# Twelve of x's sixteen row blocks turned by VectorE in 32x32 blocks, features of x and rows of w_in in another order, weights split two row blocks at a time

## The chip, the cores and the metric

The kernel runs on one core of a Trainium2 chip. A core has five engines, each with its own queue of instructions that it takes in order: TensorE (PE, matmul), VectorE (DVE), ScalarE (ACT), GpSimd (POOL) and SyncE (SP), and 16 DMA engines that carry what SP, ACT and POOL issue. The metric is the time of one execution on the device in microseconds (us). Smaller is better.

## The reference

One layer of a bidirectional encoder trunk on x of 512 tokens by 2048 features, all in float32:

```python
h = rms_norm(x, norm_w)                       # x * rsqrt(mean(x*x) + 1e-6) * norm_w
proj = jnp.einsum('bsd,de->bse', h, w_in)     # 2048 -> 4608 columns
q, k, v, g_attn, xr, g_lru = jnp.split(proj, SPLITS, axis=-1)
attn_out = attention_group(q, k, v, q_norm_w, k_norm_w)
lru_out = lru_group(xr, conv_w, conv_b, lru_wa, lru_ba, lru_wx, lru_bx, lru_lambda)
mixed = jnp.concatenate([rms_norm(attn_out, attn_norm_w) * jax.nn.silu(g_attn),
                         rms_norm(lru_out, lru_norm_w) * jax.nn.silu(g_lru)], axis=-1)
return x + jnp.einsum('bse,ed->bsd', mixed, w_out)
```

What matters here is the start: every column of `proj` is a sum over all 2048 features, so PE needs x with features on the 128 partitions (turned), and w_in with the same features on the same partitions. The order of the features is free as long as both have the same one. The factor `rsqrt(mean)` belongs to a token and is multiplied in after the matmul.

## The kernel before

**Numbers in two halves.** A float32 operand is split into a high half (rounded to the fast float32 form of PE) and a low half (the rest). A product takes three matmuls: high by high, high by low, low by high (`mm3`, lines 151 to 154: L152, L153, L154 in the profile). The high half of the weights is written by ACT (`wsplit`, L224), the low half by DVE as a subtraction (L226), each for one row block of 128 features and 512 columns, into four buffers `wh` and four `wl`.

**Chunks.** w_in is loaded in chunks of two row blocks (256 features) by 512 columns, 512 KB each (`wraw`, L203, on SP's queue), into three buffers `wr`. A projection of 512 columns goes over 8 chunks and accumulates in four PSUM banks `pj`; a chunk is 24 matmuls of 512 columns. A bank is free again when its content has been multiplied by `rbc` and stored in SBUF (`evac_bc`, L427), or scaled by `rstd` (L552).

**x.** During the first projection (columns of xr, `C_XR`) x itself is loaded and turned, chunk by chunk: `xload` (L245) brings 512 tokens by 256 features, four blocks of 128 tokens on the partitions. `xturn` lets PE turn each row block with four transpositions of 128x128 (L256) into one PSUM bank, from which ACT writes the high half, scaled by norm_w (L258), and DVE the low half (L259). `xsquare` lets DVE square the chunk and add up per token (L269). The turned halves `xh` and `xl` stay in SBUF for all later projections.

**Statistics.** When all chunks are in, `xstats` adds the sums (L306), POOL takes mean and power -0.5 (L286, L287) for `rstd`, four values per partition. In `rows` PE turns them into a row (L298), DVE copies it (L299), and POOL's queue stores it to DRAM (L301) and loads it back to all partitions as `rbc` (L302).

**What sets the order.** PE's order is that of the program text (a manual schedule for the whole kernel), as are SP's order during the first projection, POOL's up to the query projections, and ACT's and DVE's up to chunk 2. Beyond, a scheduler orders ACT and DVE by priority and its own estimate of times. In the loop of the first projection (the code is at the end of the listing) the generators `loads` and `turns` set where the loads and the turning of the later chunks are issued between PE's steps.

**Later stages.** After the first projection come a second one of xr beside the first half of the recurrence, keys and values, queries (with further buffers in a pool `wx`), then the gates beside the attention. The gate stage goes over a plan of units: `gl_units` (gate of the recurrence, in the seven products of a Strassen-like scheme, with 12 matmuls of 512 columns per chunk, some weights being sums that were put in DRAM by `two_gl` and accumulating DMAs on POOL's queue) and `ga_units` (gate of the attention, half as many columns, one of the four buffers `wh` for two row blocks). The last stage is the output projection with w_out, which has its own operands.

## Time and profile before

| | |
|---|---|
| Median of 3 runs | 642.55 us (642.46 to 642.91) |
| Span of the profiled execution | 640.7 us |
| What lies around the span, against the median | 1.85 us |
| Busy in the span: PE, DVE, ACT, POOL | 636.0, 509.9, 382.2, 131.7 us |
| First matmul of the second projection | 56.7 us after the span's start |

The profiled execution's own time is given as its span, from the first instruction to the end of the last one. Times of the timeline count from the span's start. In a row of the timeline the first number is the start and the second the length; in a row of a group stand the count, the busy time and the mean length of one in ns. A row of the stretches has, after the stretch's length, the busy time of PE, PE's weight loads, DVE, ACT and POOL, then TensorE's granted clock, the share of the DMA engines and GB/s.

### The profile page before, as it was taken

Reading aid. Unit: us, or ns where it says so; the run is one execution under the profiler, and the core shown is the slowest. Engines: PE = TensorE matmul, PEld = TensorE weight load, DVE = VectorE, ACT = ScalarE, POOL = GpSimd, SP = SyncE. Lnnn points to the kernel's source line nnn. Section 1 sums busy time; section 2 is a strip of 40 time slices with the busy share of each in tenths; the row PEclk is TensorE's granted clock in tenths of the full one; section 3 lists DMA queues with packets and bytes.
Section 4 is the critical chain, followed back from the end, with each engine's and each line's share of the span. In section 5 each row is a group of like instructions: output and inputs, shape, how many; then the busy total and the mean of one; then the engine's idle time right before and its main releaser. Section 6 shows DMA issues by size and latency. Waiting matters only on the chain.

```text
span 640.7 us, 8950 instructions
## 1 busy us (share of the span) xinstructions
PE 636.0 (99%) x2962; PEld 528.3 (82%) x2962; DVE 509.9 (80%) x886; ACT 382.2 (60%) x725; POOL 131.7 (21%) x173
## 2 busy tenths in 40 slices
PE   9999999999999999999999999999999999999997
PEld 7888888888888888888888888888888888888886
DVE  5777679996698994977678877559938988698994
ACT  3543799489954624877666775946444754344441
POOL 0013403222150501412444353322000000110000
PEclk9999999999999999999999999999999999999999
DMA  8847976897757646445989997875565857585322
GB/s 295 293 140 202 242 203 154 247 252 182 186 158 196 203 135 196 137 141 162 239 241 280 252 253 225 196 209 149 131 196 204 295 175 248 185 281 208 122 93 99
DMA packets 68782, 128.19 MB, mean 200 GB/s; under 512 B 5504, under 2 KB 24320, under 8 KB 68480
## 3 DMA queue, kind: packets, MB, share of 16 engines
q1 hardware_dynamic: 55856, 90.25, 43.2%
q0 software_dynamic: 12704, 37.23, 25.3%
q8 instruction: 23, 0.38, 0.2%
q14 instruction: 23, 0.19, 0.1%
q10 hardware_dynamic: 176, 0.14, 0.1%
HBM read 119.21 MB, written 41.95 MB: 252 GB/s over the span
## 4 chain that ended last, share of the span: by engine, by line
PE 99%; DVE 0%; issue 0%
PE pj L152 19%; PE pj L153 19%; PE pj L154 19%; PE mm L1008 13%; PE pj L1008 11%; PE mm L152 3%; PE mm L154 3%; PE mm L153 3%; PE mm L655 2%; PE mm L256 1%; PE pj L332 1%; PE pj L349 1%; PE mm L591 1%; PE mm L1253 1%; PE mm L1047 0%; PE mm L741 0%
## 5 line engine op out<-in xcount | busy, mean ns | idle before, releaser
L224 ACT CAST wh<-wr 128x512 fp32r<-128x512 f32 x151 | 90.1, 618 | 70.6 <-PE pj L154 25.4
L226 DVE TENSOR_TENSOR wl<-wr,wh 128x512 fp32r<-128x512 f32 (+1 forms) x153 | 105.6, 713 | 30.9 <-ACT wh L224 29.6
L152 PE MATMUL pj<-x,wh 128*128 128x512 f32 x240 | 95.1, 396 | 0.0
L152 PE MATMUL pj<-wh,x 128*128 128x512 f32 x240 | 93.9, 391 | 0.0
L154 PE MATMUL pj<-x,wl 128*128 128x512 f32 x240 | 93.5, 390 | 0.0
L153 PE MATMUL pj<-x,wh 128*128 128x512 f32 x240 | 93.5, 390 | 0.0
L154 PE MATMUL pj<-wh,x 128*128 128x512 f32 x240 | 93.4, 389 | 0.0
L153 PE MATMUL pj<-wl,x 128*128 128x512 f32 x240 | 93.4, 389 | 0.0
L802 ACT CAST oh<-rw 128x512 fp32r<-128x512 f32 x94 | 56.3, 621 | 38.8 <-PE mm L1008 15.5
L803 DVE TENSOR_TENSOR ol<-rw,oh 128x512 fp32r<-128x512 f32 x94 | 61.8, 687 | 10.8 <-ACT oh L802 9.2
L154 PEld LDWEIGHTS pj<-x,wl 128*128 128x128 f32 x240 | 45.0, 188 | 9.7
L154 PEld LDWEIGHTS pj<-wh,x 128*128 128x128 f32 x240 | 45.0, 188 | 9.5
L152 PEld LDWEIGHTS pj<-wh,x 128*128 128x128 f32 x240 | 45.1, 188 | 9.3
L152 PEld LDWEIGHTS pj<-x,wh 128*128 128x128 f32 x240 | 45.1, 188 | 9.2
L153 PEld LDWEIGHTS pj<-wl,x 128*128 128x128 f32 x240 | 45.1, 188 | 9.1
L153 PEld LDWEIGHTS pj<-x,wh 128*128 128x128 f32 x240 | 45.1, 188 | 8.7
L1008 PE MATMUL mm<-oh,ml 128*128 128x512 f32 (+1 forms) x128 | 49.0, 382 | 0.0
L1008 PE MATMUL mm<-ol,mh 128*128 128x512 f32 (+1 forms) x128 | 48.9, 382 | 0.0
L1008 PE MATMUL mm<-oh,mh 128*128 128x512 f32 (+1 forms) x128 | 48.9, 382 | 0.0
L940 POOL DMA_DIRECT2D out_dram<-xt x12 | 6.6, 548 | 178.7 <-DVE xt L976 129.1
L1008 PE MATMUL pj<-oh,mh 128*128 128x512 f32 (+1 forms) x104 | 39.7, 382 | 0.0
L1008 PE MATMUL pj<-ol,mh 128*128 128x512 f32 (+1 forms) x104 | 39.7, 382 | 0.0
(243 smaller groups left out, 1341.4 us busy)
## 6 DMA issues: line engine op xcount, KB each, us to landing
wr<-in_w_in_dram SPq DMA_DIRECT2D x59, 512.0 KB, 4.4
rw<-in_w_out_dram SPq DMA_DIRECT2D x63, 256.0 KB, 3.6
gs<-in_w_in_dram POOLq DMA_DIRECT2D x24, 512.0 KB, 6.8
ts<-in_w_out_dram POOLq DMA_DIRECT2D x24, 512.0 KB, 7.3
wr<-gs SPq DMA_DIRECT2D x16, 512.0 KB, 5.3
rw<-ts SPq DMA_DIRECT2D x31, 256.0 KB, 4.7
wr<-in_w_in_dram SPq DMA_DIRECT2D x17, 256.0 KB, 4.3
gs<-gs POOLq DMA_DIRECT2D x8, 512.0 KB, 7.5
```

What stands on the lines that cost most here:

```text
L152: nc.tensor.matmul(acc, lh, rh, start=start, stop=False)
L153: nc.tensor.matmul(acc, lh, rl, start=False, stop=False)
L154: nc.tensor.matmul(acc, ll, rh, start=False, stop=stop)
L224: rounded(hi[:, c], raw[:, k, c])
L226: nc.vector.tensor_sub(lo[:, c], raw[:, k, c], f(hi[:, c]))
L256: nc.tensor.transpose(pt[:, t * P : (t + 1) * P], xc[:, h * n + t, ks], ident)
L332: nc.tensor.matmul(acc[e], w[:, e * P : (e + 1) * P], x_[k], start=k == 0 and j == 0, stop=False,)
L655: nc.tensor.transpose(pt[:, s * P : (s + 1) * P], p[:, s * P : (s + 1) * P], ident)
L802: nc.scalar.copy(hi, src)
L803: nc.vector.tensor_sub(lo, src, f(hi))
L940: (queue or nc.gpsimd).dma_start(of[t * P : (t + 1) * P, os_], xts[g][t][:, cs])
L1008: nc.tensor.matmul(bank[key][:, to], lh[:, a, ts_], rh[:, cols], start=i == 0 and j == 0, stop=i == 7 and j == 2,)
```

## The change

**Features in another order.** The first four row blocks (512 features) stay as they were. The other twelve are taken in three groups of 512 features, and within a group partition p holds the features 4p to 4p+3. w_in's rows are read accordingly (`in_rows`; `two_gl` for the gate of the recurrence), and norm_w for these features comes in the same order (`nw_far`, a small load on POOL's queue).

**Turning by DVE.** For these groups `xblocks` loads x in four transfers per half group, so that 32 tokens by 32-feature strips lie on 32 partitions each; DVE's stream transposition turns the 32x32 blocks (`xfar`, two instructions of 512 elements per partition for each chunk), from SBUF to SBUF. The high and the low half are then written from SBUF, by ACT and DVE as before. The twelve groups of four transpositions on PE are gone.

**Squares on ACT.** `xsquare` (first two chunks) is done by ACT with its accumulator; for the groups `far_squares` lets ACT square 1024 elements per partition and DVE reduce them. The sums of the groups lie by strips on the partitions, so `xstats` has PE add them up with two small matmuls; mean and power follow on POOL, then the row is stored to DRAM and loaded back as `rbc` and as `rstd`.

**Weights in pairs.** `wsplit` splits both row blocks of a chunk with one ACT and one DVE instruction of 1024 elements, into two buffers of a pair each for `wh` and `wl` in place of four single ones. `ga_units` takes half of such a pair.

```diff
+    def in_rows(c, cols):
+        if c < 2:
+            return w_in[c * 2 * P : (c + 1) * 2 * P, cols].rearrange("(k p) e -> p k e", p=P)
+        w = w_in[c // 2 * 4 * P : (c // 2 + 1) * 4 * P, cols]
+        return w.rearrange("(p q) e -> p q e", q=4)[:, c % 2 * 2 : c % 2 * 2 + 2, :]
-    def wsplit(raw, k, rounded=nc.scalar.copy, parts=1):
-        turn_of[0] += k
+    def wpair():
+        turn_of[0] += 1
         pool = pools["wx" if "wx" in pools and turn_of[0] % 2 else "xw"]
-        hi = pool.tile([P, SEQ], F32R, tag="wh", bufs=4, name=nm("wh"))
-        lo = pool.tile([P, SEQ], F32R, tag="wl", bufs=4, name=nm("wl"))
+        return [pool.tile([P, 2, SEQ], F32R, tag=t, bufs=2, name=nm(t)) for t in ("wh", "wl")]
+
+    def wsplit(raw, pair, ks=slice(0, 2), rounded=nc.scalar.copy, parts=1):
+        hi, lo = pair
         cols = [slice(n * SEQ // parts, (n + 1) * SEQ // parts) for n in range(parts)]
         for c in cols:
-            rounded(hi[:, c], raw[:, k, c])
+            rounded(hi[:, ks, c], raw[:, ks, c])
         for c in cols:
-            nc.vector.tensor_sub(lo[:, c], raw[:, k, c], f(hi[:, c]))
-        return hi, lo
+            nc.vector.tensor_sub(lo[:, ks, c], raw[:, ks, c], f(hi[:, ks, c]))
+        return [(hi[:, k], lo[:, k]) for k in range(ks.start, ks.stop)]
...
     def xsquare(xc, c):
         for t in range(NT):
+            nc.scalar.activation(
+                xc[:, t, :], xc[:, t, :], AF.Square, accum_out=near[:, t, c : c + 1]
+            )
+
+    def xblocks(m, jh):
+        xb = blocks[m, jh] = b4(shape=(P, 8, P))
+        src = xf[jh * H : (jh + 1) * H, m * 4 * P : (m + 1) * 4 * P]
+        src = src.rearrange("(j r) (i f) -> i r j f", r=32, i=4)
+        for i in range(4):
+            nc.sync.dma_start(xb[32 * i : 32 * (i + 1)], src[i])
+
+    def xfar(c):
+        m, q0 = c // 2, c % 2 * 2
+        xt = b4()
+        for jh in range(2):
+            nc.vector.transpose(
+                xt[:, :, jh * H : (jh + 1) * H].rearrange("p q (j r) -> p q j r", r=32),
+                blocks[m, jh].rearrange("p j (c q) -> p q j c", q=4)[:, q0 : q0 + 2],
+            )
+        for k in range(2):
+            kk = 2 * c + k
+            xh[kk], xl[kk] = x2(), x2()
+            scale = nw_far[:, m - 1, q0 + k : q0 + k + 1]
+            nc.scalar.activation(xh[kk], xt[:, k], AF.Identity, scale=scale)
             nc.vector.scalar_tensor_tensor(
-                xc[:, t, :], xc[:, t, :], 1.0, xc[:, t, :], op0=ALU.mult, op1=ALU.mult,
-                accum_out=ssq[:, t, c : c + 1],
+                xl[kk], xt[:, k], scale, f(xh[kk]), op0=ALU.mult, op1=ALU.subtract
             )
+    def far_squares(m, jh):
+        sq = b4(shape=(P, 8, P))
+        nc.scalar.activation(sq, blocks.pop((m, jh)), AF.Square)
+        nc.vector.tensor_reduce(far[:, m - 1, jh], sq, axis=AX.X, op=ALU.add)
...
     def xstats():
...
+        nc.tensor.matmul(pt[:KT, :32], part, every, start=True, stop=False)
+        nc.tensor.matmul(
+            pt[:KT, :32], spread, every, start=False, stop=True
+        )
+        r = cut(32)[:KT]
+        nc.vector.tensor_copy(r, pt[:KT, :32])
+        nc.gpsimd.tensor_scalar(r, r, 1.0 / DM, EPS, op0=ALU.mult, op1=ALU.add)
+        nc.gpsimd.tensor_tensor(r, r, nhalf[:KT, :32], op=ALU.pow)
+        line = dp.tile([1, SEQ], F32, tag="x_line", bufs=1, name="x_line")
+        nc.gpsimd.dma_start(line.rearrange("o (j r) -> (o j) r", r=32), r)
+        nc.gpsimd.dma_start(rbc, line.broadcast_to([P, SEQ]))
+        nc.gpsimd.dma_start(rstd, line.rearrange("o (t p) -> p (o t)", p=P))
...
         c, e = step
-        if (e == 0 or e == 2) and c:
-            next(next(loads, iter(())), None)
+        if e == 0 and c:
+            for _ in range(2):
+                next(next(loads, iter(())), None)
```

More of the change, by code (lines that the diff above doesn't have):

```diff
@@ L162, in hybrid_kernel @@
     nc.gpsimd.memset(nhalf, -0.5)
-    nw_st = k2(shape=(KT, P))
-    mark = const([P, P - 16 * NT], "mark")
+    nw_st = k2(shape=(4, P))
+    mark = const([P, P - 23 * NT], "mark")
     q_r = [const([P, G], f"q_r{i}") for i in range(2 * NT)]
@@ L179, in vec_load @@
             nc.sync.dma_start(vec_st[lo : lo + src.shape[0], :], src)
-    nw = const([P, KT], "nw")
+    nw = const([P, 4], "nw")
+    nw_far = const([P, KT // 4 - 1, 4], "nw_far")
     vec = const([P, R_END], "vec")
@@ L193, in v1 @@
         return vec[:, r : r + 1]
-    def wraw(w, r0, c0, queues=(nc.sync,)):
-        raw = pools["wr"].tile([P, 2, SEQ], F32, tag="wr", bufs=3, name=nm("wr"))
-        src = w[r0 : r0 + 2 * P, c0 : c0 + SEQ].rearrange("(k p) e -> p k e", p=P)
-        nk = len(queues)
-        for k, queue in enumerate(queues):
-            ks = slice(k * 2 // nk, (k + 1) * 2 // nk)
-            queue.dma_start(raw[:, ks, :], src[:, ks, :])
-            yield raw
+    def in_rows(c, cols):
[3 more added lines that the diff above has]
+        return w.rearrange("(p q) e -> p q e", q=4)[:, c % 2 * 2 : c % 2 * 2 + 2, :]
     def wraw_first(w, r0, c0, queue):
@@ L304, in xstats, with cut @@
     def xstats():
-        s = const([P, NT], "xsum")
-        nc.vector.reduce_sum(s, ssq, axis=AX.X)
-        rsqrt_mean(rstd, s, DM, NT)
-        yield
-        rows(rbc, rstd)
+        room, at = k2(), [0]
+        def cut(n):
+            at[0] += n
+            return room[:, at[0] - n : at[0]]
+        every, which, s, part = cut(32), cut(4), cut(NT), cut(KT)
+        nc.vector.reduce_sum(every, ident.rearrange("p (i r) -> p r i", r=32), axis=AX.X)
+        nc.vector.reduce_sum(which, ident.rearrange("p (i r) -> p i r", r=32), axis=AX.X)
+        nc.vector.reduce_sum(s, near, axis=AX.X)
+        nc.vector.reduce_sum(part, far.rearrange("p m h j -> p (h j) m"), axis=AX.X)
+        spread = cut(KT)
+        nc.vector.tensor_mul(
+            spread.rearrange("p (t i) -> p t i", i=4), s[:, :, None].broadcast_to([P, NT, 4]),
+            which[:, None, :].broadcast_to([P, NT, 4]),
+        )
+        yield
+        pt = mm()
+        nc.tensor.matmul(pt[:KT, :32], part, every, start=True, stop=False)
+        nc.tensor.matmul(
+            pt[:KT, :32], spread, every, start=False, stop=True
+        )
+        r = cut(32)[:KT]
[6 more added lines that the diff above has]
+        nc.gpsimd.dma_start(rstd, line.rearrange("o (t p) -> p (o t)", p=P))
     sums_of_w = []
@@ L362, in proj_feat, with proj_tok @@
                 yield c, e
-    def tok_block(acc, w, r0, c0, lh, ll, nk):
+    def proj_tok(c0, acc):
         acc += [pj() for _ in range(NT)]
-        for c in range(nk // 2):
-            ws = wload(w, r0 + c * 2 * P, c0)
+        for c in range(KT // 2):
+            ws = wload(c, c0)
             paced(ws, c0, c)
@@ L1062, in hybrid_kernel @@
         xs, ws = xload(0, queues), wraw_first(w_in, 0, C_XR, nc.sync)
[L1063 removed]
+        nc.scalar.dma_start(nw_st, norm_w[: 4 * P].rearrange("(k p) -> k p", p=P))
+        nc.gpsimd.dma_start(nw_far, norm_w[4 * P :].rearrange("(m p q) -> p m q", p=P, q=4))
         xc, raw = next(xs), next(ws)
@@ L1069, in hybrid_kernel @@
         rest = list(xturn(xc, 0, 2))
-        first = [wsplit(raw, 0, nc.vector.tensor_copy, 2)]
+        pair = wpair()
+        first = wsplit(raw, pair, slice(0, 1), nc.vector.tensor_copy, 2)
         for r in rest:
@@ L1079, in hybrid_kernel @@
             with tc.high_priority():
-                first.append(wsplit(raw, 1))
+                first.extend(wsplit(raw, pair, slice(1, 2)))
                 turned_x(xc, 1)
@@ L1200, in gl_units @@
                         nc.vector.tensor_sub(dl, draw, f(dh))
-                    ws = [wsplit(raw, n) for n in range(2)]
+                    ws = wsplit(raw, wpair())
                 for n, (wh, wl) in enumerate(ws):
@@ L1220, in ga_units @@
                 raw = pools["wr"].tile([P, 2, SEQ], F32, tag="wr", bufs=3, name=nm("wr"))
-                src = w_in[c * 2 * P : (c + 1) * 2 * P, C_GA + part * H : C_GA + (part + 1) * H]
-                nc.sync.dma_start(raw[:, :, :H], src.rearrange("(k p) e -> p k e", p=P))
-                wh, wl = (
-                    pools["xw"].tile([P, SEQ], F32R, tag=t, bufs=4, name=nm(t)) for t in ("wh", "wl")
+                nc.sync.dma_start(
+                    raw[:, :, :H], in_rows(c, slice(C_GA + part * H, C_GA + (part + 1) * H))
                 )
-                wh, wl = (t.rearrange("p (k e) -> p k e", k=2) for t in (wh, wl))
+                wh, wl = (t[:, :, :H] for t in wpair())
                 nc.scalar.copy(wh, raw[:, :, :H])
```

46 lines of the change are left out of this document (30 added, 16 removed).

## The prediction

> **What bounds the kernel now.** The first view is the page's list of engines, with its chain that ended last.
>
> ```profile
> span 640.7 us, 8950 instructions
> PE 636.0 (99%) x2962; PEld 528.3 (82%) x2962; DVE 509.9 (80%) x886; ACT 382.2 (60%) x725; POOL 131.7 (21%) x173
> PE 99%; DVE 0%; issue 0%
> ```
>
> TensorE (PE) is busy for 636.0 of 640.7 us, and the chain is PE for 99%. So time that leaves PE leaves the kernel, and each wait that PE gets is added in full. The list of PE's waits has one row, at the start:
>
> ```profile
> PE mm L1047 <- DVE ones L159: 1.0, 1, 1.0
> ```
>
> The chain in order of time prices PE's own work (start, length):
>
> ```profile
> 16.72 2.74 PE pj L349 x12
> 30.30 0.88 PE mm L256 x8
> ```
>
> A matmul of 512 columns takes 2.74/12 = 0.228 us, a chunk of 24 takes 5.44, and one transposition 0.88/8 = 0.11. The span is 640.7 and the median of the runs 642.55; the 1.85 around the span (launch, end) are not touched, so I work with differences and add them to 642.55.
>
> No wait is no proof of slack. The timeline of the third chunk of the first projection (start, length) shows how little there is:
>
> ```profile
> 19.30 1.03 PE L256 MATMUL mm<-ident,b 128*128 128x128 f32 x8
> 19.74 1.29 DVE L226 TENSOR_TENSOR wl<-wr,wh 128x512 fp32r<-128x512 f32 x2
> 20.09 0.48 PE L152 MATMUL pj<-x,wh 128*128 128x512 f32 x1
> 20.63 0.40 PE L154 MATMUL pj<-x,wl 128*128 128x512 f32 x1
> ```
>
> The first low half is ready at 19.74 + 0.69 = 20.43, the matmul that needs it (its third) starts at 20.63. VectorE (DVE) is 0.2 us ahead, behind squares that stand before it in its queue. The stretches say the same:
>
> ```profile
> 8.00:20.00 12.00, 12.00 (x66) 10.14 (x65) 9.64 (x33) 5.43 (x10) 0.00 (x0) 1.00 0.86 298
> 20.00:40.00 20.00, 20.00 (x108) 16.91 (x106) 17.11 (x54) 10.48 (x18) 0.00 (x0) 1.00 0.83 269
> ```
>
> In these 32 us DVE (third pair) is busy for 26.75, ScalarE (ACT, fourth) for 15.91. TensorE's granted clock is 1.00, so no stall here buys a clock.
>
> **The change part by part.**
>
> *PE loses* 12 row blocks of 4 transpositions: 48 x 0.11 = 5.3 us, of which 4 blocks (1.76) stood ahead of chunk 2. The two small matmuls for the statistics replace one transposition. This is the whole possible gain.
>
> *DVE gets other work.* Prices (columns: count | busy, mean ns | idle before):
>
> ```profile
> L226 DVE TENSOR_TENSOR wl<-wr,wh 128x512 fp32r<-128x512 f32 x151 | 104.8, 716 | 30.9 <-ACT wh L224 29.6 <-PE mm L1253 1.1
> L784 DVE TENSOR_TENSOR ml<-t,mh 128x1024 fp32r<-128x1024 f32 x8 | 9.8, 1220 | 0.3 <-ACT mh L783 0.3
> L642 DVE TENSOR_REDUCE mx<-mm 128x1 f32<-128x512 f32 x32 | 21.6, 682 | 0.0
> L467 DVE SCALAR_TENSOR_TENSOR k<-ev,vec,k 128x511 f32<-128x511 f32 x16 | 11.9, 745 | 0.1
> L269 DVE SCALAR_TENSOR_TENSOR b<-b 128x256 f32<-128x256 f32 x32 | 11.9, 420 | 0.0
> L511 DVE TENSOR_TENSOR_SCAN b<-b,b 128x512 f32<-128x512 f32 x16 | 18.9, 1213 | 0.0
> L224 DVE CAST wh<-wr 128x256 fp32r<-128x256 f32 x2 | 0.6, 294 | 1.4 <-DMA wr<-in_w_in_dram 1.4
> ```
>
> Queued DVE instructions follow each other 0.08 to 0.09 us sooner than their length (two of 0.69 take 1.29 above). So from start to start: a low half of 1024 takes 1.13, a scalar_tensor_tensor of 512 0.66, a square of 256 0.35. A reduction of 1024 is not in the trace: 682 ns for 512, so as long as the 1024-wide subtraction, 1.13. No transposition by DVE is in the trace. [...] From above: a scan of 512 at 1213, 1.13 from start to start. I take 0.60, as for every other instruction that passes 512 elements once.
>
> [...]
>
> For a pair of chunks DVE did 4 scalar_tensor_tensor, 8 squares and 4 subtractions: 2.64 + 2.80 + 2.40 = 7.8 us in 12.6 us of PE time (48 matmuls, 16 transpositions). Now it does 4 transpositions, 2 reductions, 4 scalar_tensor_tensor and 2 wide subtractions: 2.40 + 2.26 + 2.64 + 2.26 = 9.6 us in 10.9. The mean still fits; the order decides. Here is DVE's queue from chunk 2 on, before (x is the turned x, high and low halves alike; b a loaded or turned block of x; ssq, near and far are sums of squares; wr, wh, wl the raw weights and their halves):
>
> ```order
> L259 SCALAR_TENSOR_TENSOR x_71_297<-mm_298,nw,x_70_296 128x512
> L259 SCALAR_TENSOR_TENSOR x_74_306<-mm_307,nw,x_73_305 128x512
> L269 SCALAR_TENSOR_TENSOR b_69_288,ssq<-b_69_288 128x256 x4
> L226 TENSOR_TENSOR wl_329<-wr_326,wh_328 128x512
> L226 TENSOR_TENSOR wl_333<-wr_326,wh_332 128x512
> ```
>
> and now, up to the low half of the same chunk:
>
> ```order
> L291 STREAM_TRANSPOSE b_67_301<-b_65_285 128x2x256
> L291 STREAM_TRANSPOSE b_75_331<-b_65_285 128x2x256
> L363 TENSOR_REDUCE k_123_560<-near 128x4
> L366 TENSOR_TENSOR k_123_560<-k_123_560 128x16
> L308 TENSOR_REDUCE far<-b_80_342 128x8
> L291 STREAM_TRANSPOSE b_67_301<-b_66_290 128x2x256
> L291 STREAM_TRANSPOSE b_75_331<-b_66_290 128x2x256
> L308 TENSOR_REDUCE far<-b_81_345 128x8
> L300 SCALAR_TENSOR_TENSOR x_69_305<-b_67_301,nw_far,x_68_304 128x512
> L300 SCALAR_TENSOR_TENSOR x_71_309<-b_67_301,nw_far,x_70_308 128x512
> L227 TENSOR_TENSOR wl_321<-wr_318,wh_320 128x1024
> ```
>
> Transpositions for both chunks of the pair and two reductions moved ahead of chunk 2's low half; between it and chunk 3's stand 4 transpositions, 2 reductions and 6 scalar_tensor_tensor: 2.40 + 2.26 + 3.96, with that low half's own 1.13 9.75 us, where PE takes 5.44 per chunk.
>
> *ACT gets the squares* and feeds that queue; its rows and the timeline it starts from:
>
> ```profile
> L783 ACT CAST mh<-t 128x1024 fp32r<-128x1024 f32 x8 | 8.4, 1053 | 5.8 <-DVE t L774 5.8
> L524 ACT ACTIVATE hsq<-hs 128x1024 f32<-128x1024 f32 x3 | 3.2, 1055 | 4.6 <-DVE hsum L525 4.6
> L494 ACT ACTIVATE b<-b,c 128x512 f32<-128x512 f32 x16 | 11.2, 744 | 0.0
> 206.97 0.31 ACT L566 ACTIVATE sh<-ev 128x128 f32<-128x128 f32 x1
> 207.40 0.31 ACT L566 ACTIVATE sh<-ev 128x128 f32<-128x128 f32 x1
> 8.10 0.69 ACT L258 ACTIVATE x<-mm,nw 128x512 fp32r<-128x512 f32 x1
> 11.34 1.27 ACT L258 ACTIVATE x<-mm,nw 128x512 fp32r<-128x512 f32 x2
> ```
>
> A square of 128 with its accumulator starts every 0.43, one of 256 some 0.54; a 1024-wide one every 0.97; a scaling of 512 from SBUF 0.62.
>
> I play the queues forward by two rules: an instruction starts when its engine is free and its inputs are there. ACT: after the scaling at 8.10 come 4 squares (8.70 to 10.84), the wide high half of chunk 1 to 11.89, two scalings to 13.0, 4 squares to 15.14, block squares done at 16.20 and 17.17. DVE: chunk 1's low half from 11.9, two scalar_tensor_tensor to 14.35, two transpositions to 15.55, then the first reduction must wait for the square until 16.24; 17.37 two transpositions, 18.57 reduction, 19.70 two scalar_tensor_tensor, 21.02 low half, ready at 22.24. PE's third matmul of chunk 2 wants it at 20.63 - 1.76 = 18.87: **3.4 us**. Then DVE 22.15: two scalar_tensor_tensor, 23.47 two transpositions, a reduction, 25.80 two, a reduction, 28.13 four scalar_tensor_tensor, 30.77 chunk 3's low half, ready 31.99. PE wants it 5.44 after the last, at 27.7: **4.3 us**. Chunk 4: 4 transpositions and 2 reductions from 31.90, one scalar_tensor_tensor, low half 37.22, ready 38.44, wanted at 37.5: **1.0**, and 0.2 for the next operand. Chunk 5's is ready at 40.2, before its time. Together 8.9.
>
> *Loads.* x comes in 24 transfers of 128 KB on SP in place of 6 of 512:
>
> ```profile
> b<-in_x_dram SPq DMA_DIRECT2D x7, 512.0 KB, 7.6
> b<-in_x_dram SPq DMA_DIRECT2D x2, 256.0 KB, 3.8
> ```
>
> Bytes and their place are the same. Each piece waits for the transfer eight before it: the last piece for chunks 2 and 3 is issued near 10.3, with the wait for chunk 1's weights, and 3.8 later is 14.1, over 3 us ahead of its transposition at 17.4. The weights of chunk 3 pass 24 issues and still have until 28.7, when ACT reaches them. I cost both at nothing; were this cover gone, they would delay DVE's row one for one.
>
> *The mean of squares* now ends in a longer chain. POOL's queue at this place before (mark paces later loads):
>
> ```order
> L286 TENSOR_SCALAR rstd<-xsum 128x4
> L287 TENSOR_TENSOR rstd<-rstd,nhalf 128x4
> L301 DMA line_632<-line_sb 4x128
> L302 DMA rbc<-line_632 128x512
> L319 COPY mark<-wl_660 128x1
> ```
>
> and now (k is the small working tile of the statistics, x_line the row in DRAM):
>
> ```order
> L378 TENSOR_SCALAR k_123_560<-k_123_560 16x32
> L379 TENSOR_TENSOR k_123_560<-k_123_560,nhalf 16x32
> L381 DMA x_line<-k_123_560 16x32
> L382 DMA rbc<-x_line 128x512
> L383 DMA rstd<-x_line 128x4x1
> ```
>
> The two POOL operations (mean and power) ran ahead of PE's step, which turned their result into a row; now they wait for PE's step and stand between its result and the row of 512 that each accumulator bank needs before it is free:
>
> ```profile
> 42.62 0.56 POOL L286 TENSOR_SCALAR rstd<-xsum 128x4 f32<-128x4 f32 x1 [41.28 <-DVE xsum L306]
> 43.26 1.04 POOL L287 TENSOR_TENSOR rstd<-rstd,nhalf 128x4 f32<-128x4 f32 x1
> 48.41 0.27 PE L298 MATMUL mm<-ident,rstd 128*4 128x128 f32 x1
> 55.50 1.89 DVE L427 TENSOR_TENSOR ev<-pj,rbc 128x512 f32<-128x512 f32 x3 [2.22 <-PE pj L154]
> 56.70 0.39 PE L152 MATMUL pj<-x,wh 128*128 128x512 f32 x1
> L287 POOL TENSOR_TENSOR rr<-rr,nhalf 128x2 f32<-128x2 f32 x4 | 4.7, 1168 | 0.3
> L674 POOL TENSOR_TENSOR asum<-asum,k 128x512 f32<-128x512 f32 x7 | 10.8, 1548 | 1.4 <-ACT k L673 1.4
> ```
>
> From 48.41 to the first evacuation's end (55.50 + 0.68) are 7.8 us, to the second projection's first matmul 8.3: slack 0.5. Added are 0.56 + 1.04 and about 0.25 for hand-overs and the second matmul: 1.85, so PE waits **1.3**. The power over 32 columns is not in the trace: over 4 it takes 1.04, over 2 no less (1168 ns), and an addition over 512 takes 1548, so I take 1.04 and keep 0.5 more as its upper end. POOL also issues a new load (nw_far) ahead of the identity:
>
> ```profile
> 1.05 0.28 POOL masks.py:199 TENSOR_SCALAR_AFFINE_SELECT ident<-ident 128x128 f32<-128x128 f32 x1
> 3.29 0.18 PEld L188 LDWEIGHTS mm<-ident,k 16*128 16x128 f32 x1 [0.41 <-issue]
> 51.61 0.61 POOL L302 DMA_DIRECT2D rbc<-line  x1 [1.36 <-DMA line<-line_sb]
> ```
>
> The identity was done at 1.33 and is first used at 3.29; an issue of 0.6 fits, so nothing.
>
> *Weights two blocks at a time* spare PE nothing. ACT and DVE save some 0.2 us per chunk, where PE is the bound. It costs lead: see the second rival.
>
> Sum: -5.3 + 8.9 + 1.3 = +4.9, and 0.4 for two more short waits like the 0.2 above: **+5.3, so 647.9 us**. Between the bounds of the transposition: at 0.35, 2 of them pass before chunk 2, 6 before chunk 3: waits 2.9, 3.4 and 0.1, sum +2.4, 645.0. At 1.13: 5.2, 6.6 and 3.2, sum +11.0, 653.6.
>
> **The rivals.**
>
> *DVE keeps up.* If the low halves come in time, only 1.3 - 5.3 is left: 638.5. For it speaks that DVE's mean load fits, 9.6 in 10.9, and that blocks land early. [...]
>
> *Pairs run dry later too.* A buffer of the gate stage was free after 6 of its chunk's 12 matmuls, now after all 12, 2.7 us before its next use; a refill is 1.05 + 1.22 = 2.3. One more instruction of 0.7 ahead of it on ACT or DVE, and PE waits 0.3. The last 12 chunks of that stage have no attention between them: 12 x 0.3 = 3.6, 651.5. For it: DVE and ACT are each busy for two thirds there:
>
> ```profile
> 404.00:440.00 36.00, 36.00 (x189) 30.05 (x188) 23.04 (x38) 24.94 (x43) 11.28 (x13) 1.00 0.68 169
> ```
>
> Against it: chunks of 24 matmuls, most of the kernel, freed their pairs at the end before too.
>
> *Transpositions at two cycles per element*, since they read every fourth word: 653.6 as above. For it: no row of this trace reads single words at a stride. [...]
>
> **How the numbers follow.** My forecast 0.62, pairs run dry 0.14, two cycles 0.12, DVE keeps up 0.07, a mixture near zero (cheap transpositions and a cheap chain) 0.05. The time is 647.9; the range 644.0 to 653.8 holds the forecast with both bounds and the second and third case. What a measurement of this kernel can tell from no change is about 0.2%, 1.3 us. Faster: 0.08; same: 0.03; slower: 0.89.
>
> **What will show it.** Right: PE's waits, nothing before, name wl and wh at the line L154 near 19, 28 and 37 us, 3 to 4 us each for the first two, with DVE busy without a gap from 17 to 40; PE's transpositions fall from 64 to 16 at L259; STREAM_TRANSPOSE has a mean near 0.69; a wait of about 1 us at the start of the second projection. Wrong: a transposition over 1 us; waits named after a DMA of x; or a PE chain still without waits.

## The result, and the profile after

The changed kernel takes 662.35 us (median of 4 runs, 660.6 to 663.38), the kernel before 642.66 (4 runs on the same chip): ratio 1.0305, 95% interval 1.0288 to 1.0322. It is slower, as forecast, but by 19.7 us where 5.3 was forecast, and it lies outside the range.

The page of the changed kernel: the list of engines, the granted TensorE clock in 40 slices of 16.5 us, and the shares of the chain that ended last.

```profile
span 659.8 us, 8656 instructions
PE 639.6 (97%) x2917; PEld 527.0 (80%) x2917; DVE 510.7 (77%) x769; ACT 383.4 (58%) x672; POOL 134.3 (20%) x175
PEclk9879799999999999999999999999999999999999
PE 80%; DMA 7%; DVE 6%; ACT 3%; issue 2%; POOL 1%; SPq 1%; DVEq 0%; ACTq 0%
```

Before, PE was 99% of the chain and the clock was full in every slice. Now 20% of the chain is other work, and the clock drops in three of the first five slices. PE is also busy for longer, 639.6 us in place of 636.0, though it has 48 transpositions (5.3 us) less to do: idle time is not the whole loss. The transpositions that PE kept, and those of DVE:

```profile
L259 PE MATMUL mm<-ident,b 128*128 128x128 f32 x16 | 2.6, 306 | 0.0
L291 DVE STREAM_TRANSPOSE b<-b 128x512 f32<-128x512 f32 x12 | 12.4, 1075 | 0.0
```

The longest rows of the list of PE's waits (in total, times, longest) are at two places:

```profile
PE pj L152 <- DVE ev L498: 5.0, 1, 5.0
PE pj L152 <- ACT wh L225: 5.0, 2, 2.9
PE pj L154 <- DVE wl L227: 3.2, 3, 1.6
```

The first row is the start of the second projection, the others are the first projection. PE's timeline (start, length) at both:

```profile
33.83 0.50 PE L152 MATMUL pj<-x,wh 128*128 128x512 f32 x1 [2.08 <-ACT wh L225]
36.18 0.80 PE L154 MATMUL pj<-x,wl 128*128 128x512 f32 x1 [1.61 <-DVE wl L227]
36.77 0.63 PE L152 MATMUL pj<-x,wh 128*128 128x512 f32 x1
37.19 0.63 PE L153 MATMUL pj<-x,wh 128*128 128x512 f32 x1
...
41.46 0.61 PE L154 MATMUL pj<-x,wl 128*128 128x512 f32 x1
...
66.13 0.39 PE L154 MATMUL pj<-x,wl 128*128 128x512 f32 x1
71.53 0.77 PE L152 MATMUL pj<-x,wh 128*128 128x512 f32 x1 [5.02 <-DVE ev L498]
72.10 0.63 PE L153 MATMUL pj<-x,wh 128*128 128x512 f32 x1
```

Behind some of these waits, matmuls of 512 columns start 0.43 us apart in place of 0.228: the granted clock is 0.50 here from 36.8 to 41.9 us and from 72.1 to 75.9, and a third time from 25.5 to 28.0; from 42 to 60 us it is 1.00. That is most of the busy time that could not be explained: some 28 matmuls at 0.2 us more each are 5.6 of the 8.9 us (3.6, and the 5.3 of the transpositions). The rest was not taken apart.

These rows give the account of the span. Before, the last matmul of the first projection started at 56.47, the first of the second at 56.70:

```profile
56.47 0.39 PE L154 MATMUL pj<-x,wl 128*128 128x512 f32 x1
```

| | us |
|---|---|
| transpositions that left PE | -5.3 |
| first projection, waits and slow matmuls: 66.13 - 56.47 + 5.3 | +15.0 |
| wait at the start of the second: 71.53 - 66.13 - 0.23 | +5.2 |
| slow matmuls behind it: ten from 71.53 to 75.94, 4.41 - 10 x 0.228 | +2.1 |
| the rest up to the end | +2.1 |
| sum: 659.8 - 640.7 | +19.1 |

DVE's timeline shows what the first projection waited for: the transpositions and the wide low halves of chunks 2, 3 and 4.

```profile
15.84 2.09 DVE L291 STREAM_TRANSPOSE b<-b 128x512 f32<-128x512 f32 x2
...
23.61 1.22 DVE L227 TENSOR_TENSOR wl<-wr,wh 128x1024 fp32r<-128x1024 f32 x1
...
34.90 1.22 DVE L227 TENSOR_TENSOR wl<-wr,wh 128x1024 fp32r<-128x1024 f32 x1
...
42.89 1.22 DVE L227 TENSOR_TENSOR wl<-wr,wh 128x1024 fp32r<-128x1024 f32 x1
```

They are ready at 24.83, 36.12 and 44.11, where I had worked out 22.24, 31.99 and 38.44. PE's longer waits name ACT's high half (L225). ACT's timeline, at chunks 1 and 3, shows that DVE stands behind them as well: the high half of chunk 3's weights comes after scalings (L299) that waited 4.56 us for transpositions.

```profile
12.29 1.05 ACT L225 CAST wh<-wr 128x1024 fp32r<-128x1024 f32 x1 [2.06 <-DMA wr<-in_w_in_dram]
...
30.29 2.56 ACT L299 ACTIVATE x<-b,nw_far 128x512 fp32r<-128x512 f32 x4 [4.56 <-DVE b L291]
32.75 1.03 ACT L225 CAST wh<-wr 128x1024 fp32r<-128x1024 f32 x1
```

The first of these rows is another matter: chunk 1's weights landed late. The same place in the kernel before:

```profile
10.27 1.14 ACT L224 CAST wh<-wr 128x512 fp32r<-128x512 f32 x2 [1.48 <-DMA wr<-in_w_in_dram]
```

And POOL's timeline shows what the second waited for:

```profile
58.81 5.48 POOL L379 TENSOR_TENSOR k<-k,nhalf 16x32 f32<-16x32 f32 x1
64.60 0.59 POOL L381 DMA_DIRECT2D x_line<-k  x1 [0.30 <-POOL k L379]
67.22 0.61 POOL L382 DMA_DIRECT2D rbc<-x_line  x1 [2.03 <-DMA x_line<-k]
```

The power over 32 columns takes 5.48 us where I took 1.04.

### The profile page after: what moved, and what is told of

Read it like the earlier page. It is cut to its first block, busy times and chain, and to the rows that moved or that the text cites. A ratio compares the mean times of both kernels' runs of the same rounds, so it can differ in the third digit from the quotient of the medians.

```text
span 659.8 us, 8656 instructions
## 1 busy us (share of the span) xinstructions
PE 639.6 (97%) x2917; PEld 527.0 (80%) x2917; DVE 510.7 (77%) x769; ACT 383.4 (58%) x672; POOL 134.3 (20%) x175
## 4 chain that ended last, share of the span: by engine, by line
PE 80%; DMA 7%; DVE 6%; ACT 3%; issue 2%; POOL 1%; SPq 1%; DVEq 0%; ACTq 0%
PE pj L154 15%; PE pj L152 15%; PE pj L153 15%; PE mm L1082 13%; PE pj L1082 10%; DMA wr<-in_w_in_dram 5%; PE mm L152 3%; PE mm L154 3%; PE mm L153 3%; DVE wl L227 2%; PE mm L726 2%; ACT wh L225 1%; POOL k L379 1%; DMA b<-in_x_dram 1%; DVE b L291 1%
## 5 line engine op out<-in xcount | busy, mean ns | idle before, releaser
L227 DVE TENSOR_TENSOR wl<-wr,wh 128x1024 fp32r<-128x1024 f32 (+2 forms) x78 | 93.4, 1198 | 34.7 <-ACT wh L225 32.2
L225 ACT CAST wh<-wr 128x1024 fp32r<-128x1024 f32 (+1 forms) x76 | 78.8, 1040 | 64.1 <-PE pj L153 21.6
L152 PE MATMUL pj<-x,wh 128*128 128x512 f32 x240 | 97.6, 407 | 10.0 <-DVE ev L498 5.0
L154 PE MATMUL pj<-x,wl 128*128 128x512 f32 x240 | 96.6, 403 | 3.2 <-DVE wl L227 3.2
L153 PE MATMUL pj<-x,wh 128*128 128x512 f32 x240 | 95.8, 399 | 0.0
L152 PE MATMUL pj<-wh,x 128*128 128x512 f32 x240 | 94.0, 392 | 0.2 <-ACT ev L623 0.2
L154 PE MATMUL pj<-wh,x 128*128 128x512 f32 x240 | 93.5, 390 | 0.0
L873 ACT CAST oh<-rw 128x512 fp32r<-128x512 f32 x94 | 56.4, 621 | 38.0 <-PE mm L1082 14.8
L152 PEld LDWEIGHTS pj<-x,wh 128*128 128x128 f32 x240 | 46.8, 195 | 20.9 <-ACT wh L225 5.8
L154 PEld LDWEIGHTS pj<-x,wl 128*128 128x128 f32 x240 | 46.6, 194 | 14.3 <-DVE wl L227 4.3
L153 PEld LDWEIGHTS pj<-x,wh 128*128 128x128 f32 x240 | 46.7, 195 | 9.8 <-DVE x L300 0.2
L152 PEld LDWEIGHTS pj<-wh,x 128*128 128x128 f32 x240 | 45.1, 188 | 10.1 <-ACT ev L623 0.8
L154 PEld LDWEIGHTS pj<-wh,x 128*128 128x128 f32 x240 | 45.0, 188 | 9.4
```

The lines of the kernel that those rows point to most:

```text
L152: nc.tensor.matmul(acc, lh, rh, start=start, stop=False)
L153: nc.tensor.matmul(acc, lh, rl, start=False, stop=False)
L154: nc.tensor.matmul(acc, ll, rh, start=False, stop=stop)
L225: rounded(hi[:, ks, c], raw[:, ks, c])
L227: nc.vector.tensor_sub(lo[:, ks, c], raw[:, ks, c], f(hi[:, ks, c]))
L873: nc.scalar.copy(hi, src)
```

## The experiments

All times are medians, beside runs of the kernel before on the same chip (its medians there were 642.66 to 643.22); the ratio is to that kernel, and differences between two kernels below are those of their ratios times 642.7. "First ends" and "second starts" are the starts of the last matmul of the first and the first matmul of the second projection in the profiled execution.

| kernel | us | ratio, 95% interval | first ends | second starts |
|---|---|---|---|---|
| before | 642.7 | 1 | 56.47 | 56.70 |
| changed | 662.35 | 1.0305 (1.0288 to 1.0322) | 66.13 | 71.53 |
| contig | 657.38 | 1.0223 (1.0207 to 1.0238) | 61.99 | 67.55 |
| tiny_turn | 654.32 | 1.0172 (1.0144 to 1.0201) | 58.95 | 64.66 |
| order_only | 654.43 | 1.0193 (1.0167 to 1.0219) | 55.57 | 63.49 |
| stats_early | 658.70 | 1.0254 (1.0234 to 1.0273) | 65.59 | 68.32 |
| after_row | 655.29 | 1.0194 (1.0171 to 1.0217) | 65.24 | 65.65 |
| delay32 | 652.07 | 1.0136 (1.0121 to 1.0152) | 57.86 | 64.56 |
| delay16 (one run) | 649.39 | | 57.41 | 61.95 |
| fill1 | 662.08 | 1.0306 (1.0292 to 1.0320) | 65.11 | 70.69 |
| fill2 | 660.86 | 1.0282 (1.0267 to 1.0297) | 64.39 | 70.02 |
| pairs_only | 649.88 | 1.0104 (1.0080 to 1.0128) | 56.69 | 56.92 |
| after_single | 659.03 | 1.0240 (1.0221 to 1.0259) | 66.10 | 70.99 |
| order_row | 648.51 | 1.0084 (1.0056 to 1.0112) | 55.78 | 56.20 |
| single_row_a | 643.81 | 1.0016 (1.0007 to 1.0025) | 57.19 | 57.62 |
| single_row_d | 641.86 | 0.9989 (0.9980 to 0.9998) | 53.31 | 53.73 |

### Why is the transposition slow?

contig lets it read contiguous words:

```diff
-                blocks[m, jh].rearrange("p j (c q) -> p q j c", q=4)[:, q0 : q0 + 2],
+                blocks[m, jh].rearrange("p j (q c) -> p q j c", q=4)[:, q0 : q0 + 2],
```

> The changed kernel, whose twelve VectorE transpositions read 32 contiguous words of each block in place of every fourth word; the features of x then meet the wrong rows of w_in, so the output is another one, with the same count of work everywhere. Theory A (the pass is slow because it reads single words at a stride of four): a transposition falls from 1.075 us to about 0.69, as other passes over 512 elements, and the waits of the first projection shrink by about half of what transpositions cost there: about 657. Theory B (a 32-bit transposition passes one element in two cycles, whatever the stride): 1.075 us stays, and the time stays at 662.

Its group of the transpositions:

```profile
L291 DVE STREAM_TRANSPOSE b<-b 128x512 f32<-128x512 f32 x12 | 7.8, 688 | 0.0
```

688 ns in place of 1075, with 512 elements and nothing else changed: theory A. The price is in the stride of four words. The time falls by 5.3 us, as expected. Two contiguous ones and the start of the next instruction lie 1.22 us apart (contig, 17.50 to 18.72), so one takes 0.61 from start to start, beside the 0.60 that the prediction took; at the stride of four words it is 2.01 for two (changed kernel, 15.84 to 17.85), 1.00 for one.

### How much of the first projection is the transposition?

tiny_turn shortens the twelve and keeps all instructions in their order:

```diff
-                xt[:, :, jh * H : (jh + 1) * H].rearrange("p q (j r) -> p q j r", r=32),
-                blocks[m, jh].rearrange("p j (c q) -> p q j c", q=4)[:, q0 : q0 + 2],
+                xt[:, :, jh * 32 : (jh + 1) * 32],
+                blocks[m, jh].rearrange("p j (c q) -> p q j c", q=4)[:, q0 : q0 + 2, 0],
```

> The changed kernel, whose twelve transpositions turn 64 elements per partition in place of 512; the halves of x then read those 64 eight times over, so the output is another one. All instructions stay, in the same order; only the length of twelve of them falls, to an estimated 0.2 us. Theory A (VectorE's queue at the first projection sets the waits, and transpositions at 1.04 us from start to start are the largest part of it): chunk 2's low half comes near 22 in place of 24.8, chunk 3's near 29.3 in place of 36.0, chunk 4's in time; waits and slow matmuls of the first projection fall from 15.1 us to about 5.5, so about 653. Rival (the two reductions and the scaled halves alone already starve TensorE): over 658. Rival (transpositions were the whole of it): 647.

654.3, near 653. Two of the short transpositions take 0.46 us, about the estimated 0.2 each. The first projection ends 7.2 us sooner; 7.8 of 15.0 remain (58.95 - 56.47 + 5.3), over the 5.5 of the expectation. The difference is a bound that comes next. ACT's timeline, at the high half of chunk 3's weights:

```profile
28.28 1.04 ACT L225 CAST wh<-wr 128x1024 fp32r<-128x1024 f32 x1 [1.79 <-DMA wr<-in_w_in_dram]
```

PE waits 3.1 us for this row. The weights of chunk 3 stand behind 24 other loads on SP's queue, 16 of them loads of x; ACT is idle for 1.79 us until they land. In the changed kernel ACT reaches that place only at 32.75, and the load has landed.

### Load or order of VectorE's queue?

order_only does the changed kernel's work with each chunk's transpositions, low half and scaled halves ahead of the reductions and squares. The loads stand in another order too: each chunk's weights are issued ahead of the next pair's blocks of x, the two rope loads later. The first step of the mean of squares, DVE's sums, comes sooner (STATS).

```diff
+TURNS = ((0, 2), (1, 1), (1, 3), (2, 2), (3, 1), (4, 0), (4, 3))
+SQUARES = {(2, 0): (1, 0), (2, 3): (1, 1), (3, 0): (2, 0), (3, 2): (2, 1), (4, 1): (3, 0), (4, 2): (3, 1)}
+STATS = ((4, 2), (6, 1))
 ...
+        given[c] = wload(c, C_XR)
 ...
-        elif jh:
-            far_squares(m, 0)
-            far_squares(m, 1)
 ...
-        if (e, c) == (2, 0) or (e == 1 and c) or (e, c) in ((3, 1), (3, 2)):
+        if (c, e) in TURNS:
             next(next(turns, iter(())), None)
+        if (c, e) in SQUARES:
+            far_squares(*SQUARES[c, e])
```

> The changed kernel with the same instructions in another order on VectorE and ScalarE: each chunk's transpositions, wide low half and scaled halves stand ahead of the reductions and squares of the blocks before, chunk by chunk; weights are loaded ahead of the blocks of the next pair; the two rope loads are issued after the last weights of the first projection. The mean of squares is left as it is. Theory A (VectorE's mean load fits with transpositions at 1.04 us: 2.08 + 1.32 + 1.13 = 4.5 of 5.44 us per chunk without the reductions, so the order sets the waits of the first projection): its waits and slow matmuls fall from 15.1 to about 2, and the 7.3 of the second projection's start stay: 662.35 - 13 = 649.4. Rival (VectorE's load itself is too much, 5.7 with a reduction per chunk): waits of 8 or more remain and are named after the low halves, over 655.

DVE's timeline, the low halves of chunks 2, 3 and 4:

```profile
18.12 1.22 DVE L231 TENSOR_TENSOR wl<-wr,wh 128x1024 fp32r<-128x1024 f32 x1 [0.31 <-ACT wh L229]
...
22.59 1.19 DVE L231 TENSOR_TENSOR wl<-wr,wh 128x1024 fp32r<-128x1024 f32 x1
...
28.13 1.19 DVE L231 TENSOR_TENSOR wl<-wr,wh 128x1024 fp32r<-128x1024 f32 x1
```

5.5, 12.3 and 14.8 us sooner than in the changed kernel, with transpositions as slow as there (a mean of 1069 ns beside 1075). The first projection ends 10.6 us sooner; of its 15.0 us 4.4 remain. So DVE's load fits and the order decides, theory A, though 2.4 us more remain than expected. The order of the loads has a part in it that was not tried alone: tiny_turn shows that chunk 3's weights would have been the next bound. The time falls by 7.2 and not by 13, because the wait behind the power grows (the power starts 7.6 us sooner, at 51.23, the first projection ends 10.6 us sooner):

```profile
PE pj L156 <- DVE ev L502: 7.5, 1, 7.5
```

### The chain behind the power

stats_early moves the two steps of the mean of squares one chunk ahead, after_row does them another way:

```diff
-        if c == KT // 2 - 2 and e in (0, 1):
+        if c == KT // 2 - 3 and e in (0, 1):
             with tc.high_priority():
                 next(stats, None)
```

> The changed kernel, with the two steps of the mean of squares one chunk earlier in TensorE's queue (chunk 5 in place of chunk 6, about 5.7 us earlier), nothing else meant to move. In the changed kernel the second projection waits 5.0 us for its first bank, because the power over 16x32 takes 5.48 us on GpSimd where I took 1.04, and after that wait ten matmuls run 0.43 us apart in place of 0.228. Theory A (a long wait costs its own length and then a slow clock): the wait and the slow matmuls both go, 662.35 - 5.0 - 2.3 = 655.0. Rival (the slow matmuls there have another cause): only the wait goes, 657.3. Rival (something else holds the banks): no change, 662.3.

```diff
+        for i in range(4):
+            nc.tensor.matmul(
+                pt[32 * i : 32 * (i + 1), :NT], every,
+                part.rearrange("p (t i) -> p i t", i=4)[:, i], start=True, stop=True,
+            )
+        nc.vector.tensor_add(s, s, pt[:, :NT])
+        rsqrt_mean(rstd, s, DM, NT)
 ...
+        nc.vector.tensor_mul(
+            diag.rearrange("p (t q) -> p t q", t=NT), ident[:, None, :].broadcast_to([P, NT, P]),
+            rstd[:, :, None].broadcast_to([P, NT, P]),
+        )
 ...
+            nc.tensor.matmul(pt[:, ts_], ones, diag[:, ts_], start=True, stop=True)
+        nc.scalar.copy(rbc, pt)
```

> The changed kernel with only the mean of squares done another way: sums to 128x4 by four small matmuls, the power on 4 columns, the row for all partitions by four matmuls of ones with a diagonal in place of the transfers. Theory A (the chain behind the power over 32 columns costs 5.0 us of wait and 2.3 of slow clock, and nothing else depends on it): 662.35 - 7.3 + 0.9 = 656.0, the second projection starts without a wait. Rival (what came early is given back by the loads or queues behind it, as stats_early gave back 3.4 of 7.3): 658 to 660.

after_row comes out at 655.3, 0.7 from theory A: without the chain the second projection starts 0.41 us after the last matmul, and 7.1 us are gone. stats_early gave only 3.3. PE's and POOL's timelines there:

```profile
65.59 0.39 PE L154 MATMUL pj<-x,wl 128*128 128x512 f32 x1
68.32 0.47 PE L152 MATMUL pj<-x,wh 128*128 128x512 f32 x1 [2.34 <-DVE ev L498]
...
69.64 0.63 PE L154 MATMUL pj<-x,wl 128*128 128x512 f32 x1
```

```profile
52.57 5.47 POOL L379 TENSOR_TENSOR k<-k,nhalf 16x32 f32<-16x32 f32 x1
58.34 0.59 POOL L381 DMA_DIRECT2D x_line<-k  x1 [0.30 <-POOL k L379]
62.43 0.61 POOL L382 DMA_DIRECT2D rbc<-x_line  x1 [3.50 <-DMA x_line<-k]
```

2.3 us of wait and seven slow matmuls remain. POOL is done with the power 6.2 us sooner, but from the issue of the row's store to that of its load pass 4.09 us, where the changed kernel had 2.62, and from there to the matmul 5.89 against 4.31. What made the two transfers slower here was not tried.

### The power and the clock, in the kernel before

delay32 and delay16 put an idle power over 32 and 16 columns into the kernel before:

```diff
         nc.vector.tensor_copy(line_sb, pt[:NT, :P])
+            nc.gpsimd.tensor_tensor(
+                idle[:NT, :slow], line_sb[:, :slow], nhalf[:NT, :slow], op=ALU.pow
+            )
```

> The kernel before, with one idle power over 4x32 on GpSimd between the row of the mean and its transfer to memory; its result is not used. It makes the row late by the length of that power and changes nothing else. Theory A (the power's length goes with its columns, and TensorE's clock falls after a wait of some us): the power takes 5.4 us, TensorE waits 5.4 - 0.5 = 4.9 us at the start of the second projection, and about ten matmuls after it run at 0.43 us in place of 0.228: 642.6 + 4.9 + 2.3 = 649.8. Rival (no clock effect): 647.5. Rival (the length goes with partitions, or the whole of 5.48 us was waiting): the power takes about 1 us, and the time is 643.2.

> The kernel before with the idle power over 4x16 in place of 4x32. Theory A (a power costs about 0.4 us and 0.16 per column, and the slow clock needs a wait of some 2 us): the power takes 2.9 us, TensorE waits 2.4 to 3.8 us at the second projection, and matmuls at 0.43 us follow only if the wait is over 2: 645 to 648. Rival (any wait brings the slow clock): ten slow matmuls whatever the wait. Rival (the power has one length for any count over 4): 5.4 us.

The powers' groups, of delay32 and of delay16:

```profile
L302 POOL TENSOR_TENSOR k<-line_sb,nhalf 4x32 f32<-4x32 f32 x1 | 5.4, 5425 | 6.8 <-DVE lc L413 6.8
```

```profile
L302 POOL TENSOR_TENSOR k<-line_sb,nhalf 4x16 f32<-4x16 f32 x1 | 2.9, 2893 | 6.4 <-DVE lc L413 6.4
```

With 1.04 over 128x4 that is 0.154 us for each further column up to 16 and 0.158 from there to 32, and over 32 columns 4 and 16 partitions take the same (5.43 and 5.48). delay32 waits 6.3 us, 1.4 more than expected, and nine matmuls at 0.43 follow the first. POOL waits 3.85 us for the row's store to land, in place of 1.36. The time grows by 8.7 us, more than the power's length; in the profiled execution the first projection ends 1.4 us later as well, so not all of it is the late row's. delay16, one run at 649.4, lies 1.4 above theory A's range: it waits 4.2 where up to 3.8 was expected, and eight matmuls 0.40 to 0.43 us apart follow.

### Does idle time bring the slow clock, and what does it cost?

fill2 and fill1 give PE matmuls of ones to do in the waits:

```diff
+    idle(40)
     fill = proj_feat(C_XR + SEQ, a2)
```

> The changed kernel with 40 matmuls of ones over 256 columns (about 0.11 us each at full clock, 4.4 us in all; their result is not used) in TensorE's queue ahead of the second projection, where it waited 5.0 us for the first bank. The wait for the bank stays where it is; TensorE is no longer idle in it. Theory A (idle time brings the slow clock): the second projection starts at the same time as before and its first ten matmuls run at 0.228 us in place of 0.43: 662.35 - 2.3 = 660.0. Rival (the slow clock comes from something else, such as the transfers): ten slow matmuls still, 662.3.

```diff
+        if (c, e) in ((1, 3), (2, 3)):
+            idle({1: 26, 2: 18}[c])
```

> The changed kernel with 26 such matmuls of ones ahead of chunk 2 (2.9 us, in its wait of 2.9) and 18 ahead of chunk 3 (2.0 us, in its wait of 2.1) of the first projection. Theory A (VectorE's queue, not TensorE, sets the end of these chunks): the slow matmuls of chunks 2 and 3 (18, some 3.6 us) go or become few, chunk 4 then waits for its low half, which is ready at 44.1 as before, and the time is 661 to 662.5. Rival (the slow clock in the first projection costs its whole length): 658.8.

In fill2 the matmuls from 70.02 on start 0.23 us apart, none is slow, though the bank came as late as before:

```profile
64.62 4.54 PE L1126 MATMUL mm<-ones 128*128 128x256 bf16 x40
70.02 0.47 PE L152 MATMUL pj<-x,wh 128*128 128x512 f32 x1 [0.85 <-DVE ev L498]
70.32 0.40 PE L153 MATMUL pj<-x,wh 128*128 128x512 f32 x1
```

So the slow clock came with the idle time here: 5.02 us of it and matmuls 0.43 us apart in the changed kernel, 0.85 and 0.23 in fill2, with no slow matmul behind it. The time falls by 1.5 us, by the two intervals something from 0 to 3 (2.3 expected; a new wait of 1.4 near 120 us takes part of it). fill1 leaves the time where it was. Of the 18 slow matmuls chunk 3's are gone, but not chunk 2's: behind 26 matmuls of ones and two of its own PE waits only 1.30 us, and eight 0.43 us apart follow.

```profile
24.02 0.57 PE L154 MATMUL pj<-x,wl 128*128 128x512 f32 x1 [1.30 <-DVE wl L227]
24.38 0.63 PE L152 MATMUL pj<-x,wh 128*128 128x512 f32 x1
24.81 0.63 PE L153 MATMUL pj<-x,wh 128*128 128x512 f32 x1
```

Why chunk 3's faster matmuls gain nothing, PE's timeline says at the third matmul of chunk 4, and DVE's at the low half of that chunk.

```profile
43.28 0.50 PE L154 MATMUL pj<-x,wl 128*128 128x512 f32 x1 [1.45 <-DVE wl L227]
```

```profile
42.02 1.20 DVE L227 TENSOR_TENSOR wl<-wr,wh 128x1024 fp32r<-128x1024 f32 x1
```

PE comes to chunk 4 sooner and waits for its low half, ready at 43.2 (44.1 in the changed kernel, where DVE's queue runs 0.9 later throughout). So in chunk 3 the slow clock costs next to nothing: DVE sets the pace there, and a slow PE only fills the waits. Behind the power no other engine holds PE, and the slow matmuls are 2.1 us of the account.

### The weights in pairs

pairs_only puts the third part of the change alone into the kernel before, after_single takes it out of the changed kernel:

```diff
-            return [wsplit(raw, k) for k in range(2)]
+            return wsplit(raw, wpair())
```

> The kernel before with only the third part of the change: weights split two row blocks at a time, in pairs of buffers, in all stages; x is turned by TensorE as before. Theory A (pairs cost a few short waits, as the changed kernel's later stages show: 0.4 near 226 us, 0.5 near 368, 0.6 near 459): 642.7 + 1 = 643.7, and the first projection keeps within 0.5 us of its time. Rival (my second rival: pairs run dry in the gate stage): 646.3 or more, with PE's waits near 430 to 450 us. Rival (the wide splits starve the first projection by themselves): waits near 19 and 28 us, over 647.

> The changed kernel with weights split one row block at a time again, as in the kernel before; all else as changed. Theory A (in the changed kernel the second projection starts 15 us later, so the loads and queues that cost 6.8 us when pairs alone were put into the kernel before have time; only the short waits seen after 220 us are the pairs'): 662.35 - 1.5 = 660.8, and the first projection keeps its waits within 1 us. Rival (the pairs cost the same 6.8 in both): 655.5. Rival (pairs help here, since they shorten VectorE's queue): over 663.

after_single came out between theory A and its first rival. Alone the pairs cost 6.7 us, as much as the rivals of pairs_only allow, but not where they said: the waits near 430 to 450 us come to 0.3, and the first projection ends as before. Theory A's 1 and both rivals' places are wrong. The largest piece is in the recurrence. PE's and ACT's timelines of pairs_only:

```profile
95.45 0.39 PE L154 MATMUL mm<-k,k 128*128 128x512 f32 x1
99.15 0.50 PE L152 MATMUL mm<-k,k 128*128 128x512 f32 x1 [3.31 <-ACT b L487]
99.48 0.40 PE L153 MATMUL mm<-k,k 128*128 128x512 f32 x1
```

```profile
92.24 0.69 ACT L487 ACTIVATE b<-mm,vec 128x512 f32<-128x512 f32 x1
96.94 0.62 ACT L460 CAST k<-k 128x512 fp32r<-128x512 f32 x1 [4.02 <-DMA k<-in_lru_wx_dram]
...
98.42 2.99 ACT L487 ACTIVATE b<-mm,vec 128x512 f32<-128x512 f32 x5
```

The scheduler, given wider splits, queued a cast of gate weights (L460) right behind the first activation, and it waits 4.0 us for its load with five activations behind it; in the kernel before that cast comes after three more of them. In the changed kernel it has the same place, but there all this runs some 15 us later and the load has landed. So what the pairs cost hangs on the queues around them: 6.7 alone, 4.2 in the changed kernel, 4.4 between order_row and single_row_a, each give or take 1.5 to 2 us by the intervals.

### Put together

order_row is order_only with after_row's mean of squares; single_row_a also undoes the pairs; single_row_d lets ACT's accumulator sum the squares of one of the six blocks.

```diff
+        if (m, jh) in ((2, 1),):
+            for j in range(8):
+                nc.scalar.activation(
+                    sq[:, j], blocks[m, jh][:, j], AF.Square,
+                    accum_out=far[:, m - 1, jh, j : j + 1],
+                )
+            return
```

> As order_only, and the mean of squares in another way: four small matmuls bring the sums to 128x4, so that the power works on 4 columns (1.04 us); the row for all partitions is then made by four matmuls of 128 columns of ones with a diagonal, and no transfer to memory and back; the constants of the recurrence are computed later. Theory A: the first projection waits about 2 us, the second starts without a wait, TensorE does 0.9 us more work, later stages keep about 1.5 us of short waits: 642.7 - 5.3 + 2 + 0.9 + 1.5 = 641.8, about as the kernel before. Rival (a wait before the second projection again, from VectorE's queue): 645 to 650.

> As single_row_d, but all six reductions by VectorE. Theory A: VectorE is the tightest engine of the first projection, so this one has some 0.5 us more of waits there: 644.0. Rival: no difference, or the accumulators cost ScalarE more than they spare VectorE and this one is faster.

> As order_row, but with weights split one row block at a time again, in the stages after as well (so the third part of the change is undone), and with the squares of one of the six blocks summed by ScalarE's accumulator in place of a reduction by VectorE. Theory A (the waits that order_row still has at 95, 107, 212 and 445 us come from the wide splits and the queues that the scheduler makes of them, 1.5 + 1.4 + 1.0 + 0.5): they go, and 648.5 - 4.5 - 0.5 = 643.5 remains, even with the kernel before or 0.2% above. Rival (they come from the other order of loads and constants): 647 to 649.

order_row came out 6.7 over theory A: the second projection starts without a wait, but waits behind ACT and DVE remain near 95, 107 and 212 us, and single_row_a, without pairs, has none of them. Added up, the three repairs fit: 1.0305 - 0.0112 (order) - 0.0111 (row) - 0.0065 (pairs) = 1.0017, and single_row_a has 1.0016; the intervals together are 0.005 wide to each side, so agreement this close is luck. The engines of single_row_d, its transpositions and the longest of its waits after the start:

```profile
PE 632.8 (99%) x2929; PEld 523.4 (82%) x2929; DVE 519.5 (81%) x842; ACT 393.7 (62%) x763; POOL 130.4 (20%) x172
```

```profile
L294 DVE STREAM_TRANSPOSE b<-b 128x512 f32<-128x512 f32 x12 | 12.5, 1078 | 0.0
```

```profile
PE pj L157 <- DVE x L304: 0.6, 3, 0.2
```

It turns the same twelve row blocks on DVE, at the same 1.08 us an instruction, and takes 641.86 us: ahead of the changed kernel by 20 us, and of the kernel before by 0.11% (interval 0.02 to 0.20%, 11 runs), which is within what was called no change. It is 1.7 us faster than single_row_a (643.5 and 644.0 were expected, 0.5 apart). That fits DVE's queue as the tightest there, where one reduction less counts.

## Why the prediction was wrong

**PE's loss of 48 transpositions, -5.3.** Right as far as the runs show: 16 are left at L259. Where hardly anything waits any more (single_row_d) PE is busy for 632.8 us, 3.2 less than before, with 0.9 of small matmuls for the mean of squares added; the other 1.2 were not taken apart.

**DVE's queue, +8.9.** The mechanism was right: waits at L152 and L154 for the high and low halves from 20 to 36 us, DVE's queue behind them, and the order in which DVE takes its work (order_only). The size was wrong: 15.0. The term that was mis-sized is the transposition, 0.60 from start to start where it takes 1.00 (2.01 for two; the expectations priced it at 1.04). Four, eight and twelve of them at 0.40 more are 1.6, 3.2 and 4.8 us of the 2.6, 4.1 and 5.7 by which chunks 2, 3 and 4 came later than worked out. The queue also began 1.5 us late behind chunk 1's weights (below); a wait of 0.7 for a square, which I had in the queue, fell away. I chose the price by "every other instruction that passes 512 elements once", and none of those rows reads single words at a stride. The upper bound, 1.13, held: with it the prediction's own waits are 5.2 + 6.6 + 3.2 = 15.0. That this is the measured 15.0 is partly luck: the bound came from a scan's length, twelve transpositions at 1.00 are 1.6 us less than at 1.13, and the late weights made up for some of it. It was also the third rival's price, to which I gave 0.12, with the right reason beside it, the stride (1075 against 688 ns); cycles per element no run shows. The lower bound of 0.35, on which the range's lower end rests, no run shows either: the runs showed 0.61 from start to start contiguous and 1.00 at the stride.

**The mean of squares, +1.3.** This step failed. The added work was counted rightly, but the power over 32 columns takes 5.48 us and not 1.04 (with it the same sum gives 5.7); the wait was 5.2, and slow matmuls behind it made it 7.3 (after_row took 7.1 of it away, with 0.9 of other work in its place). The upper end of 0.5 was no bound: it came from an addition over 512 elements, as if a power could not cost more, and from powers over 2 and 4 columns, too close together to show a slope.

**"TensorE's granted clock is 1.00, so no stall here buys a clock."** Wrong the other way round: I had asked what a stall might gain, not what it costs. Behind three waits the granted clock was 0.50. In chunk 3 of the first projection that cost next to nothing (fill1), behind the power 2.1.

**Loads, 0.** Wrong at the start. Chunk 1's weights let ACT begin their high half at 12.29 where I had worked out 10.84, and DVE's queue began 1.5 us late. A load of x of 128 KB took 6.1 us from issue to landing (median) where I took 3.8. In the other profiles with these loads of x that high half begins anywhere from 10.5 (single_row_d) to 12.2 (order_only), so the term is neither nothing nor steady; what moves it was not tried. For chunk 3's weights 0 was right in the changed kernel, and DVE was the cover: where the transpositions shrink (tiny_turn), chunk 3's weights behind the loads of x cost 3.1.

**Pairs, +0.4.** Too small: 2.1 up to the end in the account, 4.2 by after_single. The second rival named the right part, but not the place: it is in the queues that the scheduler makes, from 95 us on, not in the gate stage's buffers.

**The rivals and the range.** DVE keeps up: excluded. The range ended at 653.8, the transposition's upper bound with everything else at its middle. With 15.0 for the first projection it was used up by one term, and the power (+6.0 over the 1.3, clock included) and the pairs (+1.7 to 3.8 over the 0.4) lay outside any bound I had.

## What to carry to other kernels

A bound from the nearest row has to be of the same operation and the same access: reading every fourth word made a pass 1.6 times as long (1075 against 688 ns), and a power on GpSimd cost by its columns (2.89 us over 16, 5.43 over 32). Before a tight engine gets work in place of the bound one, look at the order of its queue and not at its mean load: here the same work in another order, with the loads in step, ended the first projection 10.6 us sooner. Price a wait of TensorE with the slow matmuls that may follow it (2.1 us behind the power), unless another engine sets the pace there anyway.
